# A transformer stack on one core: two weight sums by accumulating transfers, x scaled by its tokens early, and more tiles by seven products

## The chip, the cores and the metric

The kernel runs on one core of one Trainium2 chip. TensorE (PE) multiplies matrices, VectorE (DVE) and ScalarE (ACT) work on tiles of 128 partitions, GpSimd (POOL) does a little arithmetic and issues some transfers, SyncE (SP) issues nearly all of them. The metric is the device time of one execution in microseconds (us). The kernel before took 1914.01 us, the median of three runs (1913.86 to 1915.62).

## The reference

512 tokens of width 1024 in fp32 pass through two layers. Each layer is a half-weighted FFN, a mixer (in the first layer compressed, selected and windowed attention beside dilated attention, in the second one MLA), and another FFN. A last norm follows. All that the change touches is in the four FFNs:

```python
def _rms_norm(x, g):
    y = xf * lax.rsqrt(jnp.mean(xf * xf, axis=-1, keepdims=True) + NORM_EPS)
    return y * g
def _swiglu(x, w_gate, w_up, w_down):          # 1024 -> 2816 -> 1024
    return (jax.nn.silu(x @ w_gate) * (x @ w_up)) @ w_down
x = x + 0.5 * _swiglu(_rms_norm(x, ffn1_norm[l]), ffn1_w_gate[l], ffn1_w_up[l], ffn1_w_down[l])
```

## The kernel before

x lies transposed in SBUF: eight tiles of 128 features by 512 tokens. Every product runs as three matmuls, because each factor is split into a high part in PE's fp32r form and a low part, the difference: high by high, high by low, low by high (`mm3`, L208 to L210). ACT writes the high part (a copy into fp32r), DVE the low part (a subtraction). This holds for weights too: each weight tile comes by a transfer into a tile `w`, ACT writes `wh`, DVE writes `wl`.

An FFN (`ffn`) begins with `norm`: x times g, split into `xh` and `xl`, without the tokens' factors 1/rms. These come later as one row spread over all partitions, `rrow` (R), and DVE multiplies by R wherever a result leaves PSUM. Then the 2816 inner features go in 22 tiles of 128 (`NF`), in two halves of 11 (`HF`). For each tile gate and up are computed, then SiLU and product give `fa`, which is split into `fah` and `fal`. Behind each half comes its down phase: 88 blocks, of which each chunk `f_d` of weights (512 KB) holds eight, three matmuls of 512 columns each; eight output tiles m, each added to x with weight 0.5.

A plain tile has 48 matmuls of 512 columns: 24 for gate into the bank `pa`, 24 for up into `pb`. The other kind goes by seven products (`seven`). Gate's weights are taken as blocks A11 and A12 (upper and lower half of the features of x), up's as r21 and r22, and the tokens as two halves of 256. Seven products of such blocks then do instead of eight, 84 matmuls of 256 columns, in PE's order A11, S1, S3, S2, A12, S4, A22. Their left factors need the sums S1 = r21 + r22, S2 = S1 + A11, S3 = A11 + r21, S4 = A12 + S2; their right factors are the halves of x and combinations T of them, which `combine` makes after the first tile. DVE and ACT add up the products as they leave PSUM (tiles `fm`, `fv`, `fn`, `fg`). Tiles 4, 5, 7, 8, 10, 11, 13, 14, 16, 17, 19 and 20 go this way (`SEVEN`): mostly two in a row, then a plain one.

`fetch_seven` loads such a tile's weights by two transfers of 512 KB on SP (L170, L171) into `w` tiles, DVE makes the four sums (L174, tiles `s1` to `s4`), and ACT and DVE split seven blocks of 512 columns (L180, L181). `plan` lists all weight pieces of the program in order of use, and `chunk` fetches two pieces ahead of the one in use. The buffers in between: three `w`, three pairs of `wh` and `wl`. Where an instruction stands in its engine's queue is decided by a scheduler before the program runs, by its own estimates; each engine then works through its queue in order, and waits for whatever its first instruction needs.

Of the kernel before, what the change touches and what calls it, by code (L numbers as in the profile page):

```python
# [31 lines left out]
SEVEN = (4, 5, 7, 8, 10, 11, 13, 14, 16, 17, 19, 20)  # L32
# [45 lines left out]
class Core:  # L78
# [47 lines left out]
    def plan(self, stages):  # L126
# [15 lines left out]
        self.todo, self.ready, self.ahead = todo, [], 2  # L142
# [20 lines left out]

    def fetch_seven(self, name, l, f):

        nc, kp, sb = self.nc, self.keep, self.sb
        g, u = [kp.tile([P, 1024], F32, name="w", bufs=3) for _ in range(2)]
        nc.sync.dma_start(g, self.a[name + "_g"][l, f])  # L170
        nc.sync.dma_start(u, self.a[name + "_u"][l, f])  # L171
        a11, a12, r21, r22 = g[:, :SEQ], g[:, SEQ:], u[:, :SEQ], u[:, SEQ:]
        s1, s2, s3, s4 = [sb.tile([P, SEQ], F32, name=f"s{i}") for i in range(1, 5)]
        add = lambda o, a, b: nc.vector.tensor_tensor(o, a, b, OP.add)  # L174
        out = {}

        def parts(blocks, h, l):
            for i, (n, src) in enumerate(blocks):
                c = slice(i * SEQ, i * SEQ + SEQ)
                nc.scalar.activation(h[:, c], src, AF.Copy)  # L180
                nc.vector.tensor_tensor(l[:, c], src, raw(h[:, c]), OP.subtract)  # L181
                out[n] = h[:, c], l[:, c]

        def pair():
            return [kp.tile([P, 1024], F32R, name=n, bufs=3) for n in ("wh", "wl")]
        add(s1, r21, r22)
        add(s2, s1, a11)
        parts((("A11", a11), ("S2", s2)), *pair())
        add(s3, a11, r21)
        parts((("S1", s1), ("S3", s3)), *pair())  # L190
        add(s4, a12, s2)
        parts((("A12", a12), ("S4", s4)), *pair())
        parts((("A22", r22),), *[sb.tile([P, SEQ], F32R, name=n) for n in ("w3h", "w3l")])
        return out
# [88 lines left out]
    def combine(self, sb, gi):  # L283

        nc = self.nc
        h = [sb.tile([P, 4, SEQ], F32R, name=f"T{i}h") for i in (12, 34)]
        l = [sb.tile([P, 4, SEQ], F32R, name=f"T{i}l") for i in (12, 34)]
        a, b = slice(0, 256), slice(256, SEQ)
        for k in range(4):
            top, bot, t12, t34 = [self.tmp() for _ in range(4)]  # L290
            for t, i in ((top, k), (bot, k + 4)):
                nc.scalar.activation(t, self.x[i], AF.Copy, scale=self.g[:, gi * 8 + i:gi * 8 + i + 1])
# [3 lines left out]
            for i, t in enumerate((t12, t34)):  # L296
                nc.scalar.activation(h[i][:, k], t, AF.Copy)
                nc.vector.tensor_tensor(l[i][:, k], t, raw(h[i][:, k]), OP.subtract)
        return [(h[i // 2][:, :, c], l[i // 2][:, :, c]) for i, c in enumerate((a, b, a, b))]

    def seven(self, sb, key, xs, T, R):
# [16 lines left out]
        def t(i):  # L318
            return lambda k: (T[i][0][:, k], T[i][1][:, k])
# [19 lines left out]
        nc.vector.tensor_tensor(g, g, R, OP.mult)  # L339
# [5 lines left out]
    def ffn(self, name, l, gi, then=None):  # L345

        nc = self.nc
        with self.tc.tile_pool(name="ff", bufs=1, reuse_waits="tile") as sb:
            self.sb = sb
            xs, _, R = self.norm(gi)  # L350
            T = None
            for half in range(2):
                ah, al = [], []
                for i in range(HF):
                    f = half * HF + i
                    a = sb.tile([P, SEQ], F32, name="fa", bufs=2)
                    if f in SEVEN:
                        g, n = self.seven(sb, ("seven", name, l, f), xs, T, R)
                        nc.scalar.activation(g, g, AF.Silu)
                        nc.vector.scalar_tensor_tensor(a, n, -1.0, g, OP.mult, OP.mult)  # L360
                    else:
# [9 lines left out]
                        nc.vector.tensor_tensor(g, pgu[0], R, OP.mult)  # L371
                        nc.scalar.activation(g, g, AF.Silu)
# [7 lines left out]
                    if f == 0:  # L380
                        T = self.combine(sb, gi)
                blk, cur = 0, None
                for m in range(KT):
# [7 lines left out]
                    t = sb.tile([P, SEQ], F32, name="fg", bufs=2)  # L391
# [654 lines left out]
```

## Time and profile before

| | |
|---|---|
| median of 3 runs | 1914.01 us |
| profiled execution, its time | 1913.86 us |
| its span | 1911.7 us |
| PE busy | 1883.0 us, 98% |
| DVE busy | 1354.5 us, 71% |
| ACT busy | 903.4 us, 47% |
| POOL busy | 274.6 us, 14% |
| all transfers | 174.67 MB, mean 91 GB/s |

The span runs from the first to the last instruction of the profiled execution; its time holds a little more. Busy time is an engine's own; a share under 100% says nothing of whether the engine ever makes another wait. In a timeline neighbouring rows overlap, since an engine begins the next instruction before the last has left it: what one instruction costs in a full queue is read from start to start, not from its duration. In the rows, an arrow reads "output <- inputs", x10 is a count, and the number in brackets is the idle time ahead of an instruction with what ended it.

### The profile page before, as it was taken

The page shows a single profiled execution, that of the slowest core. Times are in us where ns is not written, and L with a number is a line of the kernel's source. Part 1 is how long each engine was busy: PE and PEld are TensorE (multiplying, and loading weights), DVE is VectorE, ACT ScalarE, POOL GpSimd, SP SyncE. Part 2 cuts the span into 40 slices and gives each one's busy share as a digit, 9 for nine tenths or more (in the row PEclk, how much of TensorE's full clock was granted, in tenths as well). Part 3 has the DMA queues.
Part 4 walks back from the last instruction along what each step waited for, and adds up shares of the span by engine and source line. Part 5 has one row for each costly group of instructions (what it writes and reads, how often), then busy time and mean ns, then how long its engine had stood idle before and what let it go on. Part 6 is the DMA issues. An engine that isn't in the chain of part 4 may idle for free. (4 is left out here: it accounts for less than half of the span.)

```text
span 1911.7 us, 27981 instructions
## 1 busy us (share of the span) xinstructions
PE 1883.0 (98%) x10850; PEld 1657.4 (87%) x10850; DVE 1354.5 (71%) x2438; ACT 903.4 (47%) x1585; POOL 274.6 (14%) x291
## 2 busy tenths in 40 slices
PE   9999999999999999999999999999999999999998
PEld 6998998878887789889988988998878879989987
DVE  8764875477888888468756864885489888747853
ACT  7432443347586654234435432443378664424432
POOL 0000000274454400000010000000156320000001
PEclk9999999999999999999999999999999999999999
DMA  4232333323111123323333232333311122333231
GB/s 170 86 113 87 110 98 109 118 89 93 58 45 34 45 85 114 100 89 109 111 92 96 82 118 89 100 108 102 123 39 33 56 89 89 111 99 100 89 110 67
DMA packets 49846, 174.67 MB, mean 91 GB/s; under 512 B 5793, under 2 KB 6049, under 8 KB 49713
## 3 DMA queue, kind: packets, MB, share of 16 engines
q1 hardware_dynamic: 48960, 171.74, 29.1%
q8 instruction: 85, 1.39, 0.3%
q10 hardware_dynamic: 720, 1.08, 0.2%
q14 instruction: 49, 0.39, 0.1%
q0 software_dynamic: 32, 0.07, 0.0%
HBM read 170.76 MB, written 2.10 MB: 90 GB/s over the span
## 5 line engine op out<-in xcount | busy, mean ns | idle before, releaser
L160 ACT ACTIVATE wh<-w 128x1024 fp32r<-128x1024 f32 (+1 forms) x217 | 229.2, 1057 | 357.7 <-PE pt L209 98.3
L161 DVE TENSOR_TENSOR wl<-w,wh 128x1024 fp32r<-128x1024 f32 (+1 forms) x217 | 273.0, 1259 | 159.4 <-ACT wh L160 158.3
L208 PE MATMUL pa<-xh,wh 128*128 128x512 f32 (+1 forms) x736 | 269.1, 366 | 2.8 <-ACT wh L160 2.2
L210 PE MATMUL pa<-xh,wl 128*128 128x512 f32 (+1 forms) x736 | 268.2, 364 | 0.5 <-DVE wl L161 0.5
L209 PE MATMUL pa<-xl,wh 128*128 128x512 f32 (+1 forms) x736 | 268.7, 365 | 0.0
L231 POOL TENSOR_TENSOR of<-of,t 128x512 f32<-128x512 f32 x36 | 55.9, 1552 | 1319.6 <-issue 892.5
L209 PE MATMUL pb<-xl,wh 128*128 128x256 f32 (+1 forms) x704 | 233.9, 332 | 0.2
L208 PE MATMUL pb<-xh,wh 128*128 128x256 f32 (+1 forms) x704 | 233.6, 332 | 0.0
L210 PE MATMUL pb<-xh,wl 128*128 128x256 f32 (+1 forms) x704 | 233.3, 331 | 0.0
L180 ACT ACTIVATE wh<-w 128x512 fp32r<-128x512 f32 x96 | 60.7, 632 | 237.9 <-PE pb L209 159.2
L208 PEld LDWEIGHTS pa<-xh,wh 128*128 128x128 f32 x736 | 139.9, 190 | 26.0 <-ACT wh L160 3.5
L210 PEld LDWEIGHTS pa<-xh,wl 128*128 128x128 f32 x736 | 139.7, 190 | 22.1 <-DVE wl L161 1.0
L209 PEld LDWEIGHTS pa<-xl,wh 128*128 128x128 f32 x736 | 139.9, 190 | 20.8 <-DVE xl L218 0.4
L209 PEld LDWEIGHTS pb<-xl,wh 128*128 128x128 f32 x704 | 133.8, 190 | 15.0 <-DVE xl L218 2.6
L208 PEld LDWEIGHTS pb<-xh,wh 128*128 128x128 f32 x704 | 133.8, 190 | 12.9 <-ACT xh L217 0.4
L210 PEld LDWEIGHTS pb<-xh,wl 128*128 128x128 f32 x704 | 133.8, 190 | 12.3
L180 ACT ACTIVATE wh<-s 128x512 fp32r<-128x512 f32 x192 | 114.9, 622 | 55.9 <-PE pa L209 26.3
L208 PE MATMUL pc<-fah,wh 128*128 128x512 f32 x352 | 137.0, 389 | 0.0
L209 PE MATMUL pc<-fal,wh 128*128 128x512 f32 x352 | 137.0, 389 | 0.0
L210 PE MATMUL pt<-fah,wl 128*128 128x512 f32 x352 | 136.9, 389 | 0.0
L210 PE MATMUL pc<-fah,wl 128*128 128x512 f32 x352 | 136.9, 389 | 0.0
L208 PE MATMUL pt<-fah,wh 128*128 128x512 f32 x352 | 136.9, 389 | 0.0
(264 smaller groups left out, 4556.3 us busy)
## 6 DMA issues: line engine op xcount, KB each, us to landing
w<-f_g SPq DMA_DIRECT2D x88, 512.0 KB, 3.7
w<-f_u SPq DMA_DIRECT2D x88, 512.0 KB, 3.6
w<-f_d SPq DMA_DIRECT2D x88, 512.0 KB, 3.7
w<-ev_in SPq DMA_DIRECT2D x16, 512.0 KB, 3.7
w<-ev_out SPq DMA_DIRECT2D x8, 512.0 KB, 3.3
w<-mla_out SPq DMA_DIRECT2D x8, 512.0 KB, 3.3
x<-x SPq DMA_DIRECT2D x8, 256.0 KB, 5.3
w<-ev_vb SPq DMA_DIRECT2D x4, 512.0 KB, 3.2
```

Source lines behind the costliest of these rows:

```text
L160: nc.scalar.activation(h[:, :cols], w[:, :cols], AF.Copy)
L161: nc.vector.tensor_tensor(l[:, :cols], w[:, :cols], raw(h[:, :cols]), OP.subtract)
L180: nc.scalar.activation(h[:, c], src, AF.Copy)
L208: nc.tensor.matmul(out, wh, xh, start=start, stop=False)
L209: nc.tensor.matmul(out, wh, xl, start=False, stop=False)
L210: nc.tensor.matmul(out, wl, xh, start=False, stop=stop)
L231: eng.tensor_tensor(parts[0], parts[0], sq, OP.add)
```

## The change

Three things change, all in the FFNs.

First, `SEVEN` becomes tiles 6 to 21: 16 of 22, all in a row from the seventh on.

Second, the weights of such a tile come in another layout, `f1_s` and `f2_s` on the chip's memory, with the four blocks side by side as A12, r22, A11, r21 (an arrangement of the input, without arithmetic). `add_up` issues two transfers: SP copies r21 into both halves of a tile `s13` (L172), and POOL then adds r22 and A11 to it in a transfer that accumulates (L174). So `s13` holds S1 and S3. There are two buffers of it, and `add_up` for the next such tile is called while the present one is fetched. A11, A12 and r22 come by three transfers of 256 KB (L190 to L192). DVE adds S2 and S4 (L204, L207), and ACT and DVE split three pairs of blocks, 1024 columns at a time, and one single block (L196, L197).

Third, x is multiplied by R itself. After the first tile `normed` forms x times g times R, and splits it; from the fourth tile on (`EARLY`) this x is used, `combine` then makes T from it into the buffers of the first `xh` and `xl`, and the multiplications by R behind PSUM go: in the tiles by seven products, in the plain tiles from the fourth on, and in the down phase, since the first three tiles get both factors of R beforehand.

```diff
-SEVEN = (4, 5, 7, 8, 10, 11, 13, 14, 16, 17, 19, 20)
+SEVEN = tuple(range(6, NF))
+EARLY = 3
 FFNS = {"f0": ("f1", 0, 0), "f1": ("f2", 0, 2), "f2": ("f1", 1, 3), "f3": ("f2", 1, 5)}
...
             else:
                 for u in flat(EVEN if st == "e" else MLA):
                     todo += keys(u)
-        self.todo, self.ready, self.ahead = todo, [], 2
+        self.todo, self.ready, self.ahead, self.sums = todo, [], 2, {}
     def fetch(self):
...
         nc.vector.tensor_tensor(l[:, :cols], w[:, :cols], raw(h[:, :cols]), OP.subtract)
         self.ready.append((key, (h, l)))
+    def add_up(self, key):
+        name, l, f = key
+        u = self.sums[key] = self.sb.tile([P, 1024], F32, name="s13", bufs=2)
+        src = self.a[name + "_s"][l, SEVEN.index(f)]
+        self.nc.sync.dma_start(u.rearrange("p (a b) -> p a b", a=2),
+                               src[:, 3 * SEQ:].unsqueeze(1).to_broadcast([P, 2, SEQ]))
+        self.nc.gpsimd.dma_start(u, src[:, SEQ:3 * SEQ], accum_op=OP.add)
     def fetch_seven(self, name, l, f):
         nc, kp, sb = self.nc, self.keep, self.sb
-        g, u = [kp.tile([P, 1024], F32, name="w", bufs=3) for _ in range(2)]
-        nc.sync.dma_start(g, self.a[name + "_g"][l, f])
-        nc.sync.dma_start(u, self.a[name + "_u"][l, f])
-        a11, a12, r21, r22 = g[:, :SEQ], g[:, SEQ:], u[:, :SEQ], u[:, SEQ:]
-        s1, s2, s3, s4 = [sb.tile([P, SEQ], F32, name=f"s{i}") for i in range(1, 5)]
-        add = lambda o, a, b: nc.vector.tensor_tensor(o, a, b, OP.add)
+        src = self.a[name + "_s"][l, SEVEN.index(f)]
+        u1, u3 = [kp.tile([P, 1024], F32, name="w", bufs=3) for _ in range(2)]
+        r22 = sb.tile([P, SEQ], F32, name="r22")
+        if not self.sums:
+            self.add_up((name, l, f))
+        u2 = self.sums.pop((name, l, f))
+        rest = [k[1:] for k in self.todo[len(self.ready) + 1:] if k[0] == "seven" and k[1:3] == (name, l)]
+        if rest:
+            self.add_up(rest[0])
+        nc.sync.dma_start(u1[:, :SEQ], src[:, 2 * SEQ:3 * SEQ])
+        nc.sync.dma_start(u3[:, :SEQ], src[:, :SEQ])
+        nc.sync.dma_start(r22, src[:, SEQ:2 * SEQ])
         out = {}
-        def parts(blocks, h, l):
-            for i, (n, src) in enumerate(blocks):
+        def parts(names, t, h, l):
+            nc.scalar.activation(h, t, AF.Copy)
+            nc.vector.tensor_tensor(l, t, raw(h), OP.subtract)
+            for i, n in enumerate(names):
                 c = slice(i * SEQ, i * SEQ + SEQ)
-                nc.scalar.activation(h[:, c], src, AF.Copy)
-                nc.vector.tensor_tensor(l[:, c], src, raw(h[:, c]), OP.subtract)
                 out[n] = h[:, c], l[:, c]
         def pair():
             return [kp.tile([P, 1024], F32R, name=n, bufs=3) for n in ("wh", "wl")]
-        add(s1, r21, r22)
-        add(s2, s1, a11)
-        parts((("A11", a11), ("S2", s2)), *pair())
-        add(s3, a11, r21)
-        parts((("S1", s1), ("S3", s3)), *pair())
-        add(s4, a12, s2)
-        parts((("A12", a12), ("S4", s4)), *pair())
-        parts((("A22", r22),), *[sb.tile([P, SEQ], F32R, name=n) for n in ("w3h", "w3l")])
+        nc.vector.tensor_tensor(u1[:, SEQ:], u2[:, :SEQ], u1[:, :SEQ], OP.add)
+        parts(("A11", "S2"), u1, *pair())
+        parts(("S1", "S3"), u2, *pair())
+        nc.vector.tensor_tensor(u3[:, SEQ:], u3[:, :SEQ], u1[:, SEQ:], OP.add)
+        parts(("A12", "S4"), u3, *pair())
+        parts(("A22",), r22, *[sb.tile([P, SEQ], F32R, name=n) for n in ("w3h", "w3l")])
         return out
     def chunk(self, *key):
...
         return xs, col, row
-    def combine(self, sb, gi):
-        nc = self.nc
-        h = [sb.tile([P, 4, SEQ], F32R, name=f"T{i}h") for i in (12, 34)]
-        l = [sb.tile([P, 4, SEQ], F32R, name=f"T{i}l") for i in (12, 34)]
+    def normed(self, sb, gi, R):
+        nc = self.nc
+        T = [[sb.tile([P, 4, SEQ], F32R, name=f"T{i}{c}") for i in (12, 34)] for c in "hl"]
+        whole, xs = [], []
+        for k in range(KT):
+            t = raw(sb.tile([P, SEQ], F32R, name="fah" if k < 4 else "fal", bufs=HF + 1))
+            nc.vector.scalar_tensor_tensor(t, self.x[k], self.g[:, gi * 8 + k:gi * 8 + k + 1], R, OP.mult, OP.mult)
+            whole.append(t)
+            h, l = [t[k // 4][:, k % 4] for t in T]
+            nc.scalar.activation(h, t, AF.Copy)
+            nc.vector.tensor_tensor(l, t, raw(h), OP.subtract)
+            xs.append((h, l))
+        return whole, xs
+    def combine(self, whole):
+        nc, kp = self.nc, self.keep
         a, b = slice(0, 256), slice(256, SEQ)
+        T = [[] for _ in range(4)]
         for k in range(4):
-            top, bot, t12, t34 = [self.tmp() for _ in range(4)]
-            for t, i in ((top, k), (bot, k + 4)):
-                nc.scalar.activation(t, self.x[i], AF.Copy, scale=self.g[:, gi * 8 + i:gi * 8 + i + 1])
+            top, bot = whole[k], whole[k + 4]
+            t12, t34 = [self.tmp() for _ in range(2)]
             for o, p, q in ((t12[:, a], top[:, b], top[:, a]), (t12[:, b], bot[:, b], t12[:, a]),
                             (t34[:, a], top[:, b], bot[:, b]), (t34[:, b], bot[:, a], t12[:, b])):
                 nc.vector.tensor_tensor(o, p, q, OP.subtract)
             for i, t in enumerate((t12, t34)):
-                nc.scalar.activation(h[i][:, k], t, AF.Copy)
-                nc.vector.tensor_tensor(l[i][:, k], t, raw(h[i][:, k]), OP.subtract)
-        return [(h[i // 2][:, :, c], l[i // 2][:, :, c]) for i, c in enumerate((a, b, a, b))]
-    def seven(self, sb, key, xs, T, R):
+                h = kp.tile([P, SEQ], F32R, name="xh", bufs=8)
+                l = kp.tile([P, SEQ], F32R, name="xl", bufs=8)
+                nc.scalar.activation(h, t, AF.Copy)
+                nc.vector.tensor_tensor(l, t, raw(h), OP.subtract)
+                for j, c in enumerate((a, b)):
+                    T[2 * i + j].append((h[:, c], l[:, c]))
+        return T
+    def seven(self, sb, key, xs, T):
         nc = self.nc
...
             return lambda k: (xs[base + k][0][:, c], xs[base + k][1][:, c])
         def t(i):
-            return lambda k: (T[i][0][:, k], T[i][1][:, k])
+            return lambda k: T[i][k]
         def twice(ap):
             return ap.unsqueeze(1).to_broadcast([P, 2, 256])
...
         prod(pb[:, a], "A12", x(4, a))
         prod(pb[:, b], "S4", x(4, b))
         nc.vector.tensor_tensor(g, m[:, :SEQ], pb, OP.add)
-        nc.vector.tensor_tensor(g, g, R, OP.mult)
         pd = self.bank("pt")
         prod(pd[:, a], "A22", t(3))
         nc.vector.tensor_tensor(n[:, a], m[:, 512:], pd[:, a], OP.subtract)
...
     def ffn(self, name, l, gi, then=None):
         nc = self.nc
         with self.tc.tile_pool(name="ff", bufs=1, reuse_waits="tile") as sb:
             self.sb = sb
             xs, _, R = self.norm(gi)
-            T = None
             for half in range(2):
                 ah, al = [], []
                 for i in range(HF):
                     f = half * HF + i
                     a = sb.tile([P, SEQ], F32, name="fa", bufs=2)
+                    if f == EARLY:
+                        xs = late
+                        T = self.combine(whole)
                     if f in SEVEN:
-                        g, n = self.seven(sb, ("seven", name, l, f), xs, T, R)
+                        g, n = self.seven(sb, ("seven", name, l, f), xs, T)
                         nc.scalar.activation(g, g, AF.Silu)
                         nc.vector.scalar_tensor_tensor(a, n, -1.0, g, OP.mult, OP.mult)
                     else:
...
                                          start=k == 0, stop=k == KT - 1)
                             pgu.append(p)
                         g = sb.tile([P, SEQ], F32, name="fg", bufs=2)
-                        nc.vector.tensor_tensor(g, pgu[0], R, OP.mult)
-                        nc.scalar.activation(g, g, AF.Silu)
+                        if f < EARLY:
+                            nc.vector.tensor_tensor(g, pgu[0], R, OP.mult)
+                            nc.scalar.activation(g, g, AF.Silu)
+                            nc.vector.tensor_tensor(g, g, R, OP.mult)
+                        else:
+                            nc.scalar.activation(g, pgu[0], AF.Silu)
                         nc.vector.tensor_tensor(a, pgu[1], g, OP.mult)
                     h = sb.tile([P, SEQ], F32R, name="fah", bufs=HF + 1)
                     lo = sb.tile([P, SEQ], F32R, name="fal", bufs=HF + 1)
...
                     ah.append(h)
                     al.append(lo)
                     if f == 0:
-                        T = self.combine(sb, gi)
+                        whole, late = self.normed(sb, gi, R)
                 blk, cur = 0, None
                 for m in range(KT):
                     p = self.bank(("pc", "pt")[m % 2])
...
                         c = slice(blk % 8 * P, blk % 8 * P + P)
                         self.mm3(p, cur[0][:, c], cur[1][:, c], ah[i], al[i], start=i == 0, stop=i == HF - 1)
                         blk += 1
-                    t = sb.tile([P, SEQ], F32, name="fg", bufs=2)
-                    nc.vector.tensor_tensor(t, p, R, OP.mult)
-                    nc.vector.scalar_tensor_tensor(self.x[m], t, 0.5, self.x[m], OP.mult, OP.add)
+                    nc.vector.scalar_tensor_tensor(self.x[m], p, 0.5, self.x[m], OP.mult, OP.add)
             if then is not None:
                 then(sb)
...
         for s, t in (("gate", "g"), ("up", "u")):
             w = i[f"ffn{n}_w_{s}"]
             d[f"f{n}_{t}"] = w.reshape(2, KT, P, NF, P).transpose(0, 3, 2, 1, 4).reshape(2, NF, P, 1024)
+        g, u = d[f"f{n}_g"][:, list(SEVEN)], d[f"f{n}_u"][:, list(SEVEN)]
+        d[f"f{n}_s"] = np.concatenate([g[..., SEQ:], u[..., SEQ:], g[..., :SEQ], u[..., :SEQ]], axis=-1)
         w = i[f"ffn{n}_w_down"].reshape(2, 2, HF, P, KT, P).transpose(0, 1, 4, 2, 3, 5)
         d[f"f{n}_d"] = w.reshape(2, 2, HF, 8, P, P).transpose(0, 1, 2, 4, 3, 5).reshape(2, 2, HF, P, 1024)
```

The scheduler gives these queues. On DVE, in the second half of the first FFN (f11 to f21; the same stands in the other three FFNs), these rows follow each other while PE works at f14. `s13_1891` belongs to f15, `s13_1759` to f14; `s13_2023` will take the buffer of `s13_1759`, as `s13_1891` took that of `s13_1706` (f13).

```order
L197 TENSOR_TENSOR wl_1899<-w_1888,wh_1898 128x1024
L204 TENSOR_TENSOR w_2020<-s13_1891,w_2020 128x512
L417 TENSOR_TENSOR fal_2016<-fa_1887,fah_2015 128x512
L364 TENSOR_TENSOR fv_2052<-fm_2053,pa_2047 128x256
L367 TENSOR_TENSOR fm_2053<-fv_2052,pt_2049 128x512
L197 TENSOR_TENSOR wl_1903<-s13_1759,wh_1902 128x1024
L207 TENSOR_TENSOR w_2021<-w_2021,w_2020 128x512
```

The sum S2 of f15 (L204) stands four places ahead of the split of S1 and S3 of f14 (L197 from `s13_1759`), and so do two evictions of products (L364, L367). Of before, these are DVE's rows in one tile by seven products of the first FFN:

```order
L174 TENSOR_TENSOR s4_2292<-w_2285,s2_2290 128x512
L181 TENSOR_TENSOR wl_2296<-w_2285,wh_2295 128x512
L181 TENSOR_TENSOR wl_2296<-s2_2290,wh_2295 128x512
L330 TENSOR_TENSOR fv_2364<-fm_2365,pa_2359 128x256
L181 TENSOR_TENSOR wl_2303<-s1_2289,wh_2302 128x512
L333 TENSOR_TENSOR fm_2365<-fv_2364,pt_2361 128x512
L181 TENSOR_TENSOR wl_2303<-s3_2291,wh_2302 128x512
L335 TENSOR_TENSOR fn_2363<-fm_2365,pt_2361 128x256
L338 TENSOR_TENSOR fg_2362<-fm_2365,pb_2360 128x512
```

There, all sums of the tile stand ahead, and no instruction in these rows waits for a transfer that one of the rows behind it releases. On SP, the same stretch of the program reads:

```order
L190 DMA w_1888<-f1_s 128x512
L192 DMA r22_1758<-f1_s 128x512
L191 DMA w_1889<-f1_s 128x512
L172 DMA s13_1891<-f1_s 128x2x512
L190 DMA w_2020<-f1_s 128x512
L192 DMA r22_1890<-f1_s 128x512
L191 DMA w_2021<-f1_s 128x512
L172 DMA s13_2023<-f1_s 128x2x512
```

Each copy into `s13` stands behind the three block transfers of an earlier tile and ahead of those of the next; before, a tile by seven products has two rows there, one for gate and one for up. On POOL the accumulating transfers of the first FFN follow each other, with only the power that makes R (L267) between the second and the third of them.

## Rows read from the trace of the kernel before

**Rows 1.** The page of before: busy times, then the clock granted in 40 slices.

```profile
PE 1883.0 (98%) x10850; PEld 1657.4 (87%) x10850; DVE 1354.5 (71%) x2438; ACT 903.4 (47%) x1585; POOL 274.6 (14%) x291
...
PEclk9999999999999999999999999999999999999999
```

**Rows 2.** Busy time by engine in stretches inside the four FFNs (columns in the first line).

```profile
core 0: us, PE busy (x) PEld busy (x) DVE busy (x) ACT busy (x) POOL busy (x), PEclk, DMA share, GB/s
57.00:341.00 284.00, 284.00 (x1726) 255.76 (x1725) 194.25 (x298) 110.46 (x168) 4.44 (x3) 1.00 0.34 102
660.00:930.00 270.00, 269.95 (x1637) 242.47 (x1636) 199.70 (x317) 117.66 (x184) 7.08 (x5) 1.00 0.32 96
...
1590.00:1875.00 285.00, 285.00 (x1733) 256.69 (x1732) 193.32 (x298) 108.41 (x164) 4.33 (x3) 1.00 0.33 100
```

**Rows 3.** PE timeline, one tile by seven products, a plain one (start, duration, instruction).

```profile
97.41 0.28 PE L208 MATMUL pa<-xh,wh 128*128 128x256 f32 x1
...
107.37 0.28 PE L210 MATMUL pt<-T34h,w3l 128*128 128x256 f32 x1
107.49 0.40 PE L208 MATMUL pa<-xh,wh 128*128 128x512 f32 x1
...
118.17 0.39 PE L210 MATMUL pb<-xh,wl 128*128 128x512 f32 x1
118.40 0.28 PE L208 MATMUL pa<-xh,wh 128*128 128x256 f32 x1
```

**Rows 4.** DVE by line and shape: count | busy, mean ns | idle before.

```profile
L339 DVE TENSOR_TENSOR fg<-fg,rrow 128x512 f32<-128x512 f32 x48 | 32.9, 685 | 0.0
...
L392 DVE TENSOR_TENSOR fg<-pc,rrow 128x512 f32<-128x512 f32 x32 | 22.1, 692 | 76.2 <-PE pc L210 75.7
L392 DVE TENSOR_TENSOR fg<-pt,rrow 128x512 f32<-128x512 f32 x32 | 22.1, 690 | 47.3 <-PE pt L210 47.3
```

**Rows 5.** The chain of waits near its end (start, us, engine, output, line).

```profile
1891.18 0.70 DVE fg L392
...
1891.90 0.70 DVE x L393
```

**Rows 6.** Timelines of ACT and PE in the first FFN: R's row; the fourth tile.

```profile
31.29 0.60 ACT L261 ACTIVATE rrow<-pt 128x512 f32<-128x512 f32 x1
...
45.85 0.39 PE L210 MATMUL pa<-xh,wl 128*128 128x512 f32 x1
```

**Rows 7.** DVE timeline inside a tile by seven products.

```profile
102.96 1.23 DVE L161 TENSOR_TENSOR wl<-w,wh 128x1024 fp32r<-128x1024 f32 x1 [1.36 <-ACT wh L160]
...
105.28 1.22 DVE L161 TENSOR_TENSOR wl<-w,wh 128x1024 fp32r<-128x1024 f32 x1
106.41 0.41 DVE L335 TENSOR_TENSOR fn<-fm,pt 128x256 f32<-128x256 f32 x1
106.74 0.68 DVE L338 TENSOR_TENSOR fg<-fm,pb 128x512 f32<-128x512 f32 x1
107.34 0.68 DVE L181 TENSOR_TENSOR wl<-w,wh 128x512 fp32r<-128x512 f32 x1
```

**Rows 8.** Transfers: all landings in w (us); a 64 KB transfer of POOL.

```profile
DMA to landing us min/median/max: 3.1/3.6/7.0
...
ident<-ident POOLq DMA_DIRECT2D x1, 64.0 KB, 3.8
```

**Rows 9.** Timelines of SP and POOL: one issue of each.

```profile
79.73 0.33 SPq L171 DMA_DIRECT2D w<-f_u  x1
...
1.23 0.76 POOL L108 DMA_DIRECT2D ident<-ident  x1 [0.79 <-POOLq L1038]
```

**Rows 10.** Timelines of ACT and DVE ahead of those starts.

```profile
101.86 1.06 ACT L160 ACTIVATE wh<-w 128x1024 fp32r<-128x1024 f32 x1 [0.99 <-PE pt L209]
...
79.02 0.69 DVE L181 TENSOR_TENSOR w3l<-w,w3h 128x512 fp32r<-128x512 f32 x1
```

**Rows 11.** What the transfers moved in the first 15 us, 40 slices.

```profile
GB/s 1 0 0 0 66 126 208 430 399 459 393 361 410 366 262 290 311 328 360 388 388 404 393 393 410 453 404 437 426 393 470 371 437 426 339 120 22 0 0 0
```


## The prediction

> **What bounds the kernel now.** I read the page first: PE is busy for 1883.0 of the 1911.7 us of the span, at the full clock in every slice [rows 1]. Then the stretches of gate, up and down work inside the four FFNs: there PE is busy without a gap (284.00 of 284.00 us), while DVE is busy for 68 to 74% and the DMA engines carry 96 to 102 GB/s [rows 2]. So in an FFN time goes by PE's columns, and another engine counts only once it makes PE wait. Then single tiles on PE. A tile by seven products runs from 97.41 to 107.49 us: 10.08 us for 84 matmuls of 256 columns, 0.120 each. The plain tile behind it runs to 118.40: 10.91 us for 48 of 512 columns, 0.227 each [rows 3]. The difference is 0.83 us a tile.
>
> **The change part by part.** Durations are those of the profiled execution (span 1911.7, its time 1913.86, which is 0.15 below the median of the runs); the sum starts at 1913.86.
>
> Tiles. 16 instead of 12 of the 22 tiles go by seven products, in four FFNs: 16 tiles x 0.83 = 13.3 us less on PE. The Trainium skill's TensorE: Matmul & The Clock Gate ("Wait — 56ns, not 53.3ns?") gives a matmul columns / 2.4 GHz + about 2.5 ns: by it 48 x 0.2158 - 84 x 0.1092 = 1.2 us a tile, an estimate, so 18.9 in all; rows 3 show 0.227 and 0.120, and they decide.
>
> Token factors in x. One multiplication of 0.68 us on DVE goes from each tile by seven products and one of 0.69 from each output block of the down phase (32 + 32 of them) [rows 4]. All lie beside PE's work except the one on the chain that ends the program, L392 at 1891.18 [rows 5]: 0.70 us less at the end. The rest is worth nothing, since PE has no gap there. What is added, x with its factors and the combinations of it, must be there when PE begins the fourth tile. In the first FFN the factors' row is written at 31.29 + 0.60 us and PE begins that tile at 45.85 [rows 6]: 14.0 us. DVE has to do 8 multiplications of x, 8 splits, and 16 half-width and 8 full combinations: 24 x 0.60 + 16 x 0.33 = 19.7 us in all by the pitches below, but only the 16 full ones of the first two kinds, 9.6 us, before PE's first product; the combinations are first used in the seventh tile. Cost: nothing.
>
> Weight sums. Before, DVE makes four sums and seven splits of 512 columns for a tile. The pitch from one DVE start to the next is 1.13 us for 1024 columns, 0.33 for 256 and 0.60 for 512 [rows 7], so with 4.0 us for the products' evictions a tile costs DVE 11 x 0.60 + 4.0 = 10.6 us. After, it is two sums, three splits of 1024 and one of 512: 1.2 + 3.4 + 0.6 + 3.4 = 8.6 us, below PE's 10.08. By busy time alone, 16 tiles in a row would be hidden and the program would end at 1913.9 - 13.3 - 0.7 = 1899.9 us.
>
> But a loop is new. s13, in which S1 and S3 are summed by transfers, has two buffers. Reloading one for tile k+2 starts when DVE's split of S1 and S3 of tile k has read it: a copy by SP, then, after that has landed, an accumulating transfer by POOL. And DVE's order has the S2 sum of tile k+2, which waits for that reload, in front of the S1 and S3 split of tile k+1 (first piece of the order). Behind the waiting sum DVE holds PE's evictions, that split, and with it the next release. So the step from release to release is L, the time of the reload, plus the DVE work from the sum to the split. For f15 that is 3 instructions of 512 columns, one of 256 and the split: 3 x 0.60 + 0.33 + 1.22 = 3.35 us. Against it stands PE's 10.08.
>
> L is not in this trace, so I bound it. Transfers of 512 KB by SP take 3.1 to 7.0 us from issue to landing, median 3.6, and a 64 KB transfer by POOL 3.8 [rows 8]. POOL's issue takes 0.76 where SP's takes 0.33 [rows 9], 0.43 more. Hops: ACT's end at 102.92 to DVE's start at 102.96, DVE's end at 79.71 to SP's at 79.73 [rows 7, 9, 10]; I allow 0.15 for all three. The low end takes both transfers at the fastest and the addition free: 3.1 + 3.1 + 0.43 + 0.15 = 6.8. The high end takes the accumulating one at the slowest: 3.6 + 7.0 + 0.43 + 0.15 = 11.2. My value takes both at the median and adds a second reading of 512 KB at the opening's 430 GB/s [rows 11], 1.2 us, and 0.2 for the three 256 KB loads of the same tile: 3.6 + 4.03 + 1.2 + 0.15 + 0.2 = 9.2. I take it because its two largest parts rest on the row with the most transfers behind it, and the other parts are small beside them.
>
> Now the loop for the second half of an FFN, tiles f11 to f21, time 0 at PE's first matmul of f11. R is the end of the split of S1 and S3. R11 can begin when PE has left the last chunk but one of the down phase, 8 blocks of 3 matmuls (5.4 us) earlier, and takes ACT's 1.06, DVE's 1.22 and hops: -2.9. From the order, each with its DVE work: R12 = R11 + L + 3.3; R13 = R12 + L + 2.15; R14 and R15 add L + 3.35 each; R15 = 4L + 9.25. PE, undelayed, wants the low part of S1 in f15 at 4 x 10.08 + 12 x 0.120 (A11) + 4 x 0.120 = 42.24. It waits 4L - 33.0. For f16 the split stands in front of the waiting sum (7.27 us of work, no L), and f17 and f18 add L + 3.95 and L + 2.42 against three tiles of PE: 2L - 16.6 more. After that the order is again harmless. The first half has f6 to f10: R9 = 3L + 5.9 against 3 x 10.08 + 1.92 = 32.16, a wait of 3L - 26.3. For one FFN 9L - 75.9, if L is over 8.75; with L under 8.25 nothing. At 9.2 it is 6.9 us, for four FFNs 27.6. Sum: 1913.9 - 13.3 - 0.7 + 27.6 = 1927.5, say **1928 us**. The low end of L gives 1900, the high end (24.9 an FFN) 1999.
>
> A rule that speaks for the other side: the Trainium skill's DMA: Bandwidth & Descriptors ("Anatomy of one DMA — SWDGE (gpsimd) path") fits a transfer issued by GpSimd as 2.0 us + bytes / 436 GB/s, 3.2 us for 512 KB. Counting the bytes twice for the addition gives 4.4, an estimate, and with 3.6 for the copy and the hops L = 8.15: no wait at all. SP's transfers show 3.6 where that fit has 3.2 [rows 8]; no run here shows POOL's.
>
> Two accumulating transfers stand in front of the token factors' power on POOL in the first three FFNs; their buffers are free by then, so I cost that at nothing, up to one reload (9 us) each if they are not.
>
> **The rivals.**
> (a) The reload is hidden and PE sets the pace: L under about 8.7. For it: the low end is 6.8, DVE's work per tile falls to 8.6 us, and DMA engines are two thirds idle [rows 2]. Against it: two landings in a row at the measured median leave only 8.7 - 2 x 3.6 - 0.43 = 1.1 us for all else. The time is 1900, up to 1910 near the threshold. This is the case on the other side: faster.
> (b) An accumulating transfer is much dearer than a copy: L from 10.2 up, 1964 at 10.2 and 1999 at 11.2. For it: POOL needed 3.8 us for only 64 KB [rows 8]. Against it: that was in the opening, where the queues are full.
> (c) Break-even: L from 8.72 to 8.93 leaves between 1910 and 1918. 0.2% (3.8 us) is about what a measurement of this kernel can tell from no change.
> (d) The new start of an FFN stalls: x with its factors comes late at the fourth tile. For it: DVE has 19.7 us of work against a window of 14.0. Each us late costs four over the FFNs: 4 us late give 1916 without the loop.
>
> **How the numbers follow.** Forecast (L 8.93 to 10.2, 1918 to 1964): 0.40. (a) 0.32. (b) 0.13. (c) 0.12. (d) 0.03, on the slower or same side. Faster 0.32, same 0.13, slower 0.55. The range: from 1898 (all of (a), with 2 us for tiles that gain a little more) to 1972, which leaves out most of (b). Since both signs hold much, the forecast's own range is 1918 to 1964.
>
> **What would show it.** If it is right, DVE's S2 sums (L204) have idle time in front of them that ends by the accumulating transfer, above all for f13 to f18; PE waits in S1 and S3 for DVE's split L197; the landing of s13 is about 3.6 for the copy and 5.2 for the accumulating one; PE's tiles keep 10.08. Wrong: no such wait, PE busy throughout the FFNs, and a program near 1900; then either L is shorter, or DVE reaches the split earlier than I place it.

## The result, and the profile after

The changed kernel takes 2032.59 us (median of 4 runs, 2029.98 to 2037.58) against 1914.42 (before, with a fourth run): ratio 1.062, 95% interval 1.0599 to 1.0641. It is slower, as forecast, but by 118 us where 14 were forecast, and outside the range. The profiled execution took 2030.01 us, with a span of 2028.2. The page of after, its busy times, clock and chain (which answer to [rows 1]):

```profile
PE 1915.7 (94%) x11426; PEld 1710.4 (84%) x11426; DVE 1330.2 (66%) x2278; ACT 913.4 (45%) x1489; POOL 327.9 (16%) x355
...
PEclk9999899999999999998999999899999999999999
...
PE 17%; DMA 4%; DVE 3%; issue 2%; ACT 0%; POOL 0%; POOLq 0%; DVEq 0%; ACTq 0%
DMA s<-f_s 3%; PE pa L224 2%; PE pa L226 2%; PE pa L225 2%; PE pt L226 1%; PE pt L225 1%; PE pt L224 1%; PE pb L225 1%; PE pb L226 1%; PE pb L224 1%; PE pc L225 1%; PE pc L224 1%; PE pc L226 1%; PE pc L478 1%; DVE wl L197 1%
```

PE now stands idle for 2028.2 - 1915.7 = 112.5 us, where it was 28.7, and a transfer is on the chain: the one into s13. What PE waited for (total us, times, longest):

```profile
PE pt L226 <- DVE wl L197: 74.7, 30, 5.0
PE pb L226 <- DVE wl L197: 8.2, 10, 1.2
```

The first row is the wait foreseen: L226 is the product with the low part, here into the bank of S1 and S3, and L197 is DVE's split. The second is the same for A12 and S4. DVE's own longest waits of that kind, and the transfers (KB each, median us to landing; [rows 8] is before):

```profile
DVE w L204 <- DMA s<-f_s: 132.6, 37, 5.6
DVE w L204 <- DMA w<-f_s: 68.1, 19, 6.5
```

```profile
s<-f_s SPq DMA_DIRECT2D x64, 512.0 KB, 4.0
s<-f_s POOLq DMA_DIRECT2D x64, 512.0 KB, 6.8
w<-f_s SPq DMA_DIRECT2D x128, 256.0 KB, 3.1
```

Two turns of the loop, on DVE (start, duration, instruction, idle before it):

```profile
195.12 1.22 DVE L197 TENSOR_TENSOR wl<-s,wh 128x1024 fp32r<-128x1024 f32 x1
...
207.63 0.69 DVE L204 TENSOR_TENSOR w<-s,w 128x512 f32<-128x512 f32 x1 [6.46 <-DMA w<-f_s]
208.24 1.22 DVE L197 TENSOR_TENSOR wl<-w,wh 128x1024 fp32r<-128x1024 f32 x1
209.38 0.42 DVE L364 TENSOR_TENSOR fv<-fm,pa 128x256 f32<-128x256 f32 x1
209.71 1.22 DVE L197 TENSOR_TENSOR wl<-s,wh 128x1024 fp32r<-128x1024 f32 x1
...
222.44 0.69 DVE L204 TENSOR_TENSOR w<-s,w 128x512 f32<-128x512 f32 x1 [3.10 <-DMA s<-f_s]
223.05 0.41 DVE L364 TENSOR_TENSOR fv<-fm,pa 128x256 f32<-128x256 f32 x1
223.38 1.22 DVE L197 TENSOR_TENSOR wl<-s,wh 128x1024 fp32r<-128x1024 f32 x1
```

The split of f11 ends at 196.34, and the sum that needs its buffer again starts at 207.63: L is 11.3 us. (The last thing that this sum waited for was a load into w, which came at about the same time as the transfer into s13.) The next turn, which ends by s13 alone, has 210.93 to 222.44, 11.5. Over the 36 turns that the prediction's formula counts, the mean is 11.4. From split to split it is 14.6 and 13.7 us, against PE's 10.08. The two transfers of the first turn, on SP and POOL:

```profile
196.36 0.38 SPq L172 DMA_DIRECT2D s<-f_s  x1
200.58 0.86 POOL L174 DMA_DIRECT2D s<-f_s  x1 [65.28 <-DMA s<-f_s]
```

The copy lands 3.7 us after its issue, POOL issues the addition 0.5 us after that landing, and the addition lands 6.8 us after its own issue.

The second part of the loss stands in the clock. Three stretches of after, and PE behind two of the waits:

```profile
core 0: us, PE busy (x) PEld busy (x) DVE busy (x) ACT busy (x) POOL busy (x), PEclk, DMA share, GB/s
40.00:62.00 22.00, 22.00 (x99) 18.22 (x98) 22.00 (x40) 11.90 (x18) 0.00 (x0) 1.00 0.28 85
...
215.00:230.00 15.00, 12.90 (x92) 12.64 (x93) 10.35 (x16) 6.51 (x10) 1.73 (x2) 0.89 0.55 141
230.00:245.00 15.00, 12.23 (x82) 12.02 (x82) 8.87 (x13) 4.94 (x8) 0.86 (x1) 0.79 0.55 136
```

```profile
224.65 0.39 PE L226 MATMUL pt<-xh,wl 128*128 128x256 f32 x1 [2.10 <-DVE wl L197]
...
236.31 0.28 PE L224 MATMUL pb<-T34h,wh 128*128 128x256 f32 x1
236.43 0.28 PE L225 MATMUL pb<-T34l,wh 128*128 128x256 f32 x1
239.48 0.58 PE L226 MATMUL pt<-xh,wl 128*128 128x256 f32 x1 [2.77 <-DVE wl L197]
239.86 0.41 PE L224 MATMUL pt<-xh,wh 128*128 128x256 f32 x1
...
242.85 0.41 PE L226 MATMUL pt<-xh,wl 128*128 128x256 f32 x1
```

Ahead of the wait the pitch is 0.120 us; behind it 14 pitches from 239.86 to 242.85 take 0.214 each, 256 columns at 1.2 GHz, the lower of the two levels. PE had waited 2.10 and 2.77 us in the 18 us before. In the stretches of [rows 2] PE of before waited 0.05 us in all, and the clock stood at 1.00. The first of the three stretches shows that the new start of the first FFN costs nothing: PE is busy throughout around the fourth tile.

### The profile page after: what moved, and what is told of

It reads as the page before. It is cut to its first block, busy times and chain, and to the rows that moved or that the text cites. A ratio compares the mean times of both kernels' runs of the same rounds, so it can differ in the third digit from the quotient of the medians.

```text
span 2028.2 us, 29506 instructions
## 1 busy us (share of the span) xinstructions
PE 1915.7 (94%) x11426; PEld 1710.4 (84%) x11426; DVE 1330.2 (66%) x2278; ACT 913.4 (45%) x1489; POOL 327.9 (16%) x355
## 5 line engine op out<-in xcount | busy, mean ns | idle before, releaser
L174 POOL DMA_DIRECT2D s<-f_s x64 | 55.8, 876 | 1098.7 <-DMA s<-f_s 314.2
L226 PE MATMUL pt<-xh,wl 128*128 128x256 f32 x512 | 162.3, 317 | 74.7 <-DVE wl L197 74.7
L226 PE MATMUL pa<-xh,wl 128*128 128x512 f32 (+1 forms) x576 | 199.0, 346 | 0.0
L196 ACT ACTIVATE wh<-w 128x1024 fp32r<-128x1024 f32 x128 | 135.3, 1057 | 139.6 <-PE pt L225 48.0
L226 PEld LDWEIGHTS pt<-xh,wl 128*128 128x128 f32 x512 | 112.4, 220 | 80.8 <-DVE wl L197 80.8
L197 DVE TENSOR_TENSOR wl<-w,wh 128x1024 fp32r<-128x1024 f32 x128 | 156.4, 1222 | 33.9 <-ACT wh L196 33.9
L204 DVE TENSOR_TENSOR w<-s,w 128x512 f32<-128x512 f32 x64 | 44.3, 692 | 200.7 <-DMA s<-f_s 132.6
L226 PE MATMUL pb<-T34h,wl 128*128 128x256 f32 (+1 forms) x560 | 166.1, 297 | 8.3 <-DVE wl L197 8.2
L224 PE MATMUL pb<-T34h,wh 128*128 128x256 f32 (+1 forms) x560 | 165.0, 295 | 0.0
L225 PE MATMUL pb<-T34l,wh 128*128 128x256 f32 (+1 forms) x560 | 164.5, 294 | 0.0
L225 PE MATMUL pt<-xl,wh 128*128 128x256 f32 x512 | 157.8, 308 | 0.0
L224 PE MATMUL pt<-xh,wh 128*128 128x256 f32 x512 | 157.5, 308 | 0.0
L226 PE MATMUL pc<-fah,wl 128*128 128x512 f32 x352 | 136.9, 389 | 0.0
L225 PE MATMUL pt<-fal,wh 128*128 128x512 f32 x352 | 136.9, 389 | 0.0
```

Source lines behind the costliest of these rows:

```text
L174: self.nc.gpsimd.dma_start(u, src[:, SEQ:3 * SEQ], accum_op=OP.add)
L196: nc.scalar.activation(h, t, AF.Copy)
L197: nc.vector.tensor_tensor(l, t, raw(h), OP.subtract)
L204: nc.vector.tensor_tensor(u1[:, SEQ:], u2[:, :SEQ], u1[:, :SEQ], OP.add)
L224: nc.tensor.matmul(out, wh, xh, start=start, stop=False)
L225: nc.tensor.matmul(out, wh, xl, start=False, stop=False)
```

## The experiments

Ratios are to the kernel before, run on the same chip, each with its 95% interval.

**1. The sum behind the split.** One edge more in the order that the scheduler makes; transfers, buffers and tiles as in the change.

```diff
+        with self.tc.issue_after(self.cut):   # split of S1, S3 of the tile before
+            nc.vector.tensor_tensor(u1[:, SEQ:], u2[:, :SEQ], u1[:, :SEQ], OP.add)
```

> The changed kernel with one edge more: DVE's S2 sum of the next tile is queued behind the split of S1 and S3 of the tile before it, instead of ahead of it. Transfers, buffers and tiles are the same. Theory (loop): PE lost time because the sum, waiting about 11.3 us for the reload of s13, held back the split that releases the other buffer; with the split first, two reloads overlap, a pair of tiles needs about 11.3 + 6 us against 20.2 us of PE, so PE's waits for the split go from 83 us to under 10 and the time is 1897 to 1910. Rival (contention): the accumulating transfers slow every load, whatever the order: about 2030. Rival (density): 16 tiles in a row are too much for DVE: about 2030.

1910.94 us, ratio 0.9975 (0.9963 to 0.9986): 122 us less than the change by the order alone, with the accumulating transfer as slow as before (6.9 us). DVE's rows at the same point of the program, then PE's waits for the split and DVE's for s13 in the whole run:

```profile
208.59 1.22 DVE L198 TENSOR_TENSOR wl<-s,wh 128x1024 fp32r<-128x1024 f32 x1
209.72 0.68 DVE L207 TENSOR_TENSOR w<-s,w 128x512 f32<-128x512 f32 x1
...
218.91 1.22 DVE L198 TENSOR_TENSOR wl<-s,wh 128x1024 fp32r<-128x1024 f32 x1
220.34 0.69 DVE L207 TENSOR_TENSOR w<-s,w 128x512 f32<-128x512 f32 x1 [0.21 <-DMA s<-f_s]
...
223.95 0.69 DVE L217 TENSOR_TENSOR w<-w 128x512 f32<-128x512 f32 x1
```

```profile
PE pb L236 <- DVE wl L198: 5.9, 7, 1.2
DVE w L207 <- DMA s<-f_s: 45.8, 33, 3.4
```

The step is 10.3 us, and PE's waits for the split go from 83 us to 5.9. Contention and density fall as causes of the loss. The edge moved more than the one sum: the S4 sum (L217 here) now stands behind the splits of A12 and A22, where in the change (L207) it stood ahead of them. This run does not separate the two sums; in the change the S4 sum waited 25.9 us for loads, the S2 sum 200.7. The time is 1 us above the range expected: something of about 11 us is left.

**2. Three buffers.**

```diff
-        u = ... name="s13", bufs=2)
+        u = ... name="s13", bufs=3)          # fah, fal: HF + 1 -> HF
```

> The changed kernel with three buffers for s13 instead of two (room for it comes from one buffer less each of fah and fal, 11 instead of 12). DVE's order keeps the sum ahead of the split. Theory (loop): the buffer that the sum waits for was released a tile earlier, so two tiles need 11.3 + 3.3 us against 20.2 of PE: 1897 to 1910, no wait for the split over 1 us. Contention or density: about 2030.

1942.03 us, 1.014 (1.0123 to 1.0157): 91 us less than the change, but above the 1910 expected, and 42 above experiment 9, which has the third buffer and the new order. PE's wait for s13's split goes (74.7 to 1.6 us). What is left is a wait for the split of A12 and S4, and the sums now wait for the plain loads in w:

```profile
PE pb L226 <- DVE wl L197: 18.5, 25, 1.6
DVE w L204 <- DMA w<-f_s: 77.9, 32, 5.7
DVE w L207 <- DMA w<-f_s: 70.3, 51, 3.3
```

Those buffers, too, are released by splits that stand behind a waiting sum. The third buffer opens the loop through s13 and leaves the one through w; the order opened both.

**3. No addition.**

```diff
-        self.nc.gpsimd.dma_start(u, src[:, SEQ:3 * SEQ], accum_op=OP.add)
+        self.nc.gpsimd.dma_start(u, src[:, SEQ:3 * SEQ])
```

> The changed kernel with POOL's transfer a plain copy over s13 instead of an addition into it (so S1 and S3 are not the sums; what is computed there is left out). Same bytes read from memory, same order, same buffers. Theory (loop, and the addition is the dear part): POOL's transfer lands in 4.0 to 4.6 us instead of 6.8, the reload takes 8.2 to 9.0 us, and by 9 x L - 75.9 an FFN the time is 1900 to 1920. If a transfer issued by POOL is dear by itself: still 6 us or more to landing, and over 1980. Density: about 2030.

1943.36 us, 1.0144 (1.0129 to 1.0159). POOL's plain copy lands in 4.8 us and SP's in 3.8:

```profile
s<-f_s SPq DMA_DIRECT2D x64, 512.0 KB, 3.8
s<-f_s POOLq DMA_DIRECT2D x64, 512.0 KB, 4.8
```

So POOL costs 1.0 us over SP (0.43 was estimated) and the addition 6.8 - 4.8 = 2.0 (1.2 was estimated). The time is well above the 1900 to 1920 expected. The reload took 8.5 to 10.7 us, mean 9.24 over the 36 turns that the formula counts, and 4 x (9 x 9.24 - 75.9) is 29 us. PE's wait is this:

```profile
PE pt L226 <- DVE wl L197: 26.5, 20, 3.1
```

So the formula gives the wait rightly here. The rest is in PE's busy time, 1884.8 us where experiment 9 has 1870.5 for the same matmuls: 14.3 us that no term of the formula holds.

**4. The sums on DVE, 16 tiles, x with its factors.**

```diff
-    add_up and the fetch_seven of after
+    fetch_seven of before (two loads, four adds, seven splits of 512)
```

> The changed kernel with the weights loaded and summed as before the change (two loads of 512 KB, four sums and seven splits of 512 columns on DVE), but 16 tiles by seven products and x with its tokens' factors. No transfer by POOL. Theory (loop): DVE needs 11 x 0.60 + 3.4 = 10.0 us a tile against PE's 10.08, so it just keeps up: 1898 to 1915. Density: DVE falls behind in 11 tiles in a row, over 1930. Contention: 1900.

1911.4 us, 0.9976 (0.9965 to 0.9987): no loss without the transfers, and only 4.4 us of gain. Why it stays 11 us above experiment 11, which has only 0.2 us less of DVE's work in a tile, stays open. Compared matmul by matmul, about 5 of the 11 us come in the second mixer, which neither edit touches.

**5. 12 tiles with the transfers.**

```diff
-SEVEN = tuple(range(6, NF))
+SEVEN = (4, 5, 7, 8, 10, 11, 13, 14, 16, 17, 19, 20)
```

> The changed kernel with the 12 tiles by seven products of before (4, 5, 7, 8, 10, 11, 13, 14, 16, 17, 19, 20) instead of 16: copies and accumulating transfers, x with its tokens' factors. Theory (loop): two such tiles and a plain one give PE 31.1 us for two reloads, 15.5 us each, against a step of 11.3 + 2.2 to 3.4 us, so most of the wait goes: 1913 to 1930. Rival (contention, the accumulating transfers slow all loads): 12/16 of the loss of the change stays, about 2000.

1935.21 us, 1.0098 (1.0083 to 1.0113), above the range. It is not the loop: PE waits 1.2 us in all for DVE's split L197, in three waits, of which this is the longest:

```profile
PE pb L226 <- DVE wl L197: 0.7, 1, 0.7
```

The next run shows where the time goes.

**6. The token factors alone** (before's tiles and sums, x by `normed`).

```diff
-SEVEN = tuple(range(6, NF))
+SEVEN = (4, 5, 7, 8, 10, 11, 13, 14, 16, 17, 19, 20)   # and fetch_seven of before
```

> The kernel before with one part of the change alone: x with its tokens' factors from the fourth tile on, and no multiplications by them afterwards. Tiles and sums as before. If this part costs nothing but the 0.7 us that it saves at the end: ratio 0.998 to 1.001. If it is what kept the fourth experiment from its 14 us (the new start of an FFN delays PE in some of the four FFNs): 1.001 to 1.004.

1939.43 us, 1.0121 (1.0106 to 1.0136), more than either theory gave. Tiles by seven products begin here at the fifth, and PE waits in it and the next for DVE's split of the combinations:

```profile
PE pt L212 <- DVE xl L317: 4.2, 5, 1.1
```

Beside it are many short waits in the fifth and sixth tile; in the first FFN they, PE's restarts and a spell at the lower clock add up to 8 us before 75 us, in which DVE is full (30.88 of 31 us busy from 44 to 75). So the factored x is free only where such tiles begin late enough, as in the change. It also reads the fifth run: with the same tiles the transfers (1935) are no dearer than the sums on DVE (1939). That the plain tile in between is what gives the reload its time was not tested by itself.

**7. 16 tiles alone.**

```diff
-SEVEN = (4, 5, 7, 8, 10, 11, 13, 14, 16, 17, 19, 20)
+SEVEN = tuple(range(6, NF))                             # in the kernel before
```

> The kernel before with one part of the change alone: tiles 6 to 21 by seven products. DVE still multiplies by the tokens' factors, 10.6 us a tile against PE's 10.08. If DVE's work a tile sets the pace, it falls behind by 0.5 us in each of 11 tiles and the gain of 3.3 us an FFN is gone: 1912 to 1925. If the buffers between hide that: 1900 to 1908.

1914.42 us, 0.999 (0.9981 to 0.9999): DVE sets the pace. Late in the second half of the first FFN PE starts tiles 10.75 us apart, each time after a wait:

```profile
265.90 0.28 PE L209 MATMUL pb<-xl,wh 128*128 128x256 f32 x1
266.60 0.39 PE L208 MATMUL pa<-xh,wh 128*128 128x256 f32 x1 [0.41 <-ACT wh L180]
266.82 0.28 PE L209 MATMUL pa<-xl,wh 128*128 128x256 f32 x1
...
277.35 0.39 PE L208 MATMUL pa<-xh,wh 128*128 128x256 f32 x1 [0.41 <-ACT wh L180]
...
288.10 0.39 PE L208 MATMUL pa<-xh,wh 128*128 128x256 f32 x1 [0.41 <-ACT wh L180]
```

The wait is for ACT, but ACT is busy for 5.53 of these 10.75 us, PE for 10.34 and DVE for all of them:

```profile
266.60:277.35 10.75, 10.34 (x84) 10.13 (x85) 10.75 (x21) 5.53 (x11) 0.00 (x0) 1.00 0.35 101
```

So DVE's work in a tile, 10.6 us by the prediction and 10.75 here, is the limit, and relieving DVE was needed. PE makes 12 such waits in the whole run, 5.0 us; the earlier tiles of each half do not wait.

**8. Wide splits, sums on DVE, single buffers for r22 and s13.**

```diff
+        nc.sync.dma_start(u1, src[:, 2 * SEQ:])                            # A11, r21
+        nc.vector.tensor_tensor(u2[:, :SEQ], r22, u1[:, SEQ:], OP.add)        # S1
+        nc.vector.tensor_tensor(u2[:, SEQ:], u1[:, :SEQ], u1[:, SEQ:], OP.add)  # S3
```

> A version meant to beat both: 16 tiles, x with its tokens' factors, no transfer by POOL. Weights come by one load of 512 KB (A11 and r21) and two of 256 KB, DVE makes all four sums (S1 and S3 into one tile, S2 in place of r21), and ACT and DVE split 1024 columns at a time as in the changed kernel. DVE needs 4 x 0.60 + 3 x 1.13 + 0.60 + 3.4 = 9.8 us a tile. Theory (nothing in this kernel waits for a transfer that DVE itself holds back): no waits beyond 5 us, 1898 to 1908. If 16 tiles in a row bring waits of their own on ACT's and DVE's queues, as the fourth experiment's 1911 suggests: 1908 to 1916.

1972.21 us, 1.0297 (1.028 to 1.0314): the same fault without any POOL transfer. S1's sum waits for r22, whose single buffer DVE itself releases with its last split, and ACT waits for the sum:

```profile
DVE s L186 <- DMA r<-f_s: 40.3, 31, 3.0
```

```profile
ACT wh L178 <- DVE w L188: 194.4, 45, 5.5
```

**9. Experiment 1 with three buffers.**

```diff
+        with self.tc.issue_after(self.cut): ...   # and s13 bufs=3, fah, fal: HF
```

> The first experiment (S2 sum behind the split) with three buffers for s13 as in the second. Theory: what the first experiment left over (1911 where 1900 was hoped for) is DVE still waiting for s13 and for the loads in w, 71 us of waits in front of the sums; with the third buffer s13 comes a tile earlier, the waits for it go, and the time is 1900 to 1906. Rival: the leftover is that of 16 such tiles in a row, as in the fourth experiment, which has no s13 and took 1911: 1908 to 1913.

1900.45 us, 0.9922 (0.9908 to 0.9937). PE's page row, and its stretch in the second half of the first FFN, where after has 180.91 us busy in 195:

```profile
PE 1870.5 (98%) x11426; PEld 1675.1 (88%) x11426; DVE 1328.9 (70%) x2278; ACT 917.1 (48%) x1489; POOL 329.9 (17%) x355
```

```profile
189.00:360.00 171.00, 171.00 (x1193) 160.70 (x1191) 119.16 (x165) 77.96 (x102) 16.34 (x19) 1.00 0.51 139
```

PE is busy throughout, with the accumulating transfers in place. DVE no longer waits for s13 at all, where it still waited 45.8 us in the first experiment; that fits what was left there, and the rival, 16 such tiles in a row, is out.

**10. Experiment 1 with a buffer of its own for A12.**

```diff
-        u1, u3 = [kp.tile(..., name="w", bufs=3) for _ in range(2)]
+        u1 = kp.tile(..., name="w", bufs=3); u3 = sb.tile([P, 1024], F32, name="u3")
```

> The first experiment with A12 and S4 in a buffer of their own, so that the three buffers of w hold A11 and S2 alone (room from one buffer less each of fah and fal). In the second experiment the wait had moved to the loads in w (148 us in front of S2 and S4). Theory (those loads also hold the first experiment back): waits of DVE for w go from 25 us to under 5, 1900 to 1907. Rival: A12's single buffer is reloaded too late, or the leftover lies elsewhere: 1909 to 1916.

1939.67 us, 1.0122 (1.0105 to 1.0139), worse than either theory's range: one buffer is too few, and DVE's S4 sum waits for its reload. The S2 sum's waits for w, foreseen under 5 us, are 11.2.

```profile
DVE u L218 <- DMA u<-f_s: 101.4, 56, 5.8
```

**11. Wide splits, two loads, two buffers.**

```diff
+        nc.sync.dma_start(u1, src[:, 2 * SEQ:])     # A11, r21
+        nc.sync.dma_start(u3, src[:, :2 * SEQ])     # A12, r22; s13, w3h, w3l: bufs=2
```

> The eighth experiment's idea without its single buffers: two loads of 512 KB a tile (A11 with r21, A12 with r22), four sums on DVE (S1 and S3 into one of two buffers, S2 in place of r21, S4 in place of r22 after A22 is split), splits of 1024 columns, two buffers for A22's parts. No transfer by POOL; DVE needs 9.8 us a tile. Theory (the eighth lost its time because S1's sum waited for r22's single buffer, which DVE's own last split of the tile before releases): without that release loop 1900 to 1912. Rival (splits of 1024 columns make PE wait longer for a tile's first weights, whatever the buffers): about 1970.

1900.43 us, 0.992 (0.9905 to 0.9934). Against the eighth, the buffers, the way of loading and the place of A22's split (now ahead of the S4 sum) differ, and 72 us with them; which of them counts was not separated. This version takes 0.8% less than the kernel before, as experiment 9 does, without a transfer by POOL.

**12. The same with 17 tiles.**

```diff
-SEVEN = tuple(range(6, NF))
+SEVEN = tuple(range(5, NF))
```

> The eleventh experiment with 17 tiles by seven products, 5 to 21 instead of 6 to 21. If the combinations of x are ready by the sixth tile: 4 x 0.83 = 3.3 us less, 1897. In the sixth experiment, where such tiles begin at the fifth, PE waits in them for the combinations (up to 1.1 us a time for L317); if that reaches the sixth tile too: 1900 to 1910.

1901.54 us, 0.9932 (0.9915 to 0.9948): no gain. For the combinations PE does not wait. It begins to wait for weights: in the first FFN twice 0.44 us for ACT's L177, in the second and fourth for DVE's split:

```profile
PE pa L209 <- DVE wl L178: 3.4, 5, 1.4
```

Experiment 11 has 0.3 us of that wait.

## Why the prediction was wrong

*Tiles, 13.3 us less: right.* With the loop open, PE's busy time is 1870.5 (experiment 9) where 1883.0 - 13.3 = 1869.7 was foreseen, and the time falls by 15.5 us (12 to 18 by the interval), 14.0 foreseen.

*The 0.7 at the end: wrong.* From the start of PE's last FFN matmul to DVE's first row of the output it is 5.16 us before (1898.23 to 1903.39) and 5.17 in experiment 9 (1885.19 to 1890.36). In both PE works on for 2.82 of them without a gap, on transposes and the last norm's sums, before its product with the last squares; DVE's multiplication lay beside that.

*The start of an FFN costs nothing: right*, since tiles by seven products begin at the seventh; with the fifth it costs (experiment 6). Rival (d) is out: in experiment 9 PE's idle time is 28.5 us, that of before 28.7.

*DVE below PE's pace: right* (experiments 7 and 9).

*The loop: right in its place and kind.* DVE's order held the releasing split behind the waiting sum; the new order took 122 us away (experiment 1). From the step's own working, R15 - R11 is 4L + 12.15 = 57.4 us at L = 11.3; the trace has 195.12 to 252.37, 57.3, between these splits. Rival (a), that PE sets the pace, is out, and so is (c).

*The step that failed is the size of L.* "My value takes both at the median" gave 9.2, and its high end 11.2; measured are 11.3 to 11.5 in the turns shown and 11.4 in the mean, just over that end. The copy took 4.0 us instead of 3.6, POOL's plain transfer 4.8 instead of 4.03 and the addition 2.0 instead of 1.2 (experiment 3). From the copy's landing to POOL's issue it is 0.5 us, where 0.15 was allowed for all three hops; the prediction had no row of such a hop. The sum for the other side, L = 8.15, took 3.2 us for POOL's copy and falls with the 4.8. Rival (b) is what happened, and it had a chance of 0.13; its 1999 is still 34 us short. By 9L - 75.9, L = 11.4 gives 26.7 us an FFN and 1899.9 + 107 = 2007.

*The rest is a term that the sum did not have:* it held PE's pitch ("PE's tiles keep 10.08"). Against experiment 9, which runs the same transfers, the span is 129.2 us longer: PE idle 112.5 - 28.5 = 84.0, and PE busy 1915.7 - 1870.5 = 45.2 for the same matmuls. The mean granted clock is 0.975, in experiment 9 0.995: 2.5% of 2028.2 less 0.5% of 1899.0 is 41 us. That is an estimate from above, since PE also waits in some of the stretches at the lower level. Counted in the trace, 359 matmuls of 256 columns run in such stretches and cost 35 us over a pitch of 0.120; in experiment 9 it is 11 and 1.3 us. The Trainium skill's TensorE: Matmul & The Clock Gate gives columns / 1.2 GHz for a matmul at the lower level ("Wait — 56ns, not 53.3ns?"), 0.213 us for 256 columns; the trace agrees with 0.214. The clock is not all: experiment 2 has the same 0.995 as experiment 9 and still 1886.9 us of PE busy, 16.4 more, behind many short waits. And the waits are 84 us and not the formula's 107, though the formula holds in experiment 3; that a slower PE asks later, and so waits less, is an argument that no run tests. No run held the clock up with the waits in place, so how the two parts depend on each other stays open.

## What to carry to other kernels

Ask of every instruction that waits for a reload whether the release of the next reload stands behind it on the same in-order engine: then the step is the reload plus that work. Busy time does not show it. One more buffer may not be enough: here it took away 91 us, the order 122, and both together brought the time to 1900. Price a wait on PE twice, once as time (84 us here) and once as the slower matmuls behind it (45). Where a transfer's duration decides and no row has its kind, let the range reach well past the slowest neighbour, since four small underestimates (0.4 to 0.8 us each) made 2.2 us of L and some 79 us here by the formula.

## What was not expected of the hardware

A 512 KB transfer issued by POOL landed in 4.8 us where SP's took 3.8, and 6.8 when it accumulates; POOL's issue itself went from 0.53 to 0.86 us with the addition. PE fell to the lower clock behind single waits of 2 to 4 us, but not behind each: after one of 2.63 us that ends at 780.34 the granted clock is 0.57 from 781 to 785 us, and around one of 2.71 us that ends at 915.51 it stays at 1.00. And a short wait costs PE more than its length in the rows: in experiment 7 a wait of 0.41 us makes one pitch 0.70 us instead of 0.12 (265.90 to 266.60) and the next 0.22.
